# The first expert's rows by a product of the tokens on chip with a selection matrix, in place of a gather through DRAM and transposes

## The chip, the cores and the metric

The kernel runs on one core of a Trainium2 chip, as one program in one launch. The metric is the device time of one execution in microseconds. Engines are named as in the profile: PE (matmuls; PEld is its weight load), DVE, ACT, POOL and SP, which issues most of the DMAs. A profile covers one execution, and its times are counted from the start of that execution's span.

## The reference, cut to what matters

Two blocks run one after the other on 512 tokens of 1024 channels: a mixer block of two layers, and a second block with two kinds of attention and a mixture of experts. Only the mixture of experts and the step that leads into it matter here.

```python
x = x + jnp.concatenate([o_dil, o_fox], axis=-1) @ w_out[layer]
h2 = _rmsnorm(x, ffn_norm[layer]).reshape(B * T, D)
...
group_probs = jax.nn.softmax(group_logits, axis=-1)
g1, g_idx = lax.top_k(group_probs, 1)
sel = jnp.take_along_axis(expert_logits, g_idx[:, :, None], axis=1)[:, 0]
top_v, top_i = lax.top_k(sel, TOP_K_IN_GROUP)
g2 = jax.nn.softmax(top_v, axis=-1)
...
for e in range(N_EXPERTS):
    he = jax.nn.silu(xt @ w_gate[e]) * (xt @ w_up[e])
    y = y + combine[:, e:e + 1] * (he @ w_down[e])
```

There are 32 experts in 4 groups. Each token goes to two experts of one group. An expert has two matrices of 1024 x 256 (gate, up) and one of 256 x 1024 (down), in float32: 3 MB per expert, about 100 MB in all.

## The kernel before, in words

**Instructions and their order.** The program is traced in Python. A scheduler then orders the instructions of each engine by what they depend on and by the order in which they were traced. Inside a block `manual_schedule` the instructions of the engines named keep the order in which they are traced (others may be put between them). `issue_after(ins)` puts all that is traced in it behind `ins` on the engine of `ins`. Each engine, and each DMA queue, works in order.

**The step into the experts** is `second_out` (L1458). The 512 tokens are four tiles of 128 tokens on the partitions. For each tile a generator `tile(t)` (L1482) makes the two halves of the output projection (`pfo`), adds them into the tokens `xk` on chip, sums the squares, transposes the tokens (`turn8`, L1500) for the router, takes `rs`, the tile's inverse root mean square (`rsq`, L1501), and makes the router's logits (`plg`, L1505). Then ACT writes the scaled tokens in another channel order to `h` (L1509), which goes to the DRAM tensor `h2d` (L1510). `route_tile` (L1550) picks the two experts of each token (`both` has a 1 for each) on DVE. PE then counts how many earlier tokens chose the same expert (`prank`, L1583 and L1584), which gives the token's place among the expert's rows, and sums the table of tokens by place and expert in PSUM (`ppos`, L1592). The steps of the four tiles are interleaved by hand: `SO[0]` in free order, `SO[1] = (3,0,3,1,3,2,3,1,2,3,2,3)` under `manual_schedule` for PE, so PE's last steps are `prank` of tile 3, `ppos` of tile 2, `ppos` of tile 3.

**From the tables to the experts.** `route_end` (L1633) reads the table of the first three experts (`tables_of`, L1598 and L1599), which gives `tok`, the token numbers in the order of the rows. `sort_experts` (L1640) is traced under `issue_after(self.tabled.ins)` (L1991), so its DVE part comes behind those two instructions. It counts the tokens of each expert (`pcnt`), forms keys (L1652), compares all pairs (`sx`, L1654), sums to a `rank` (L1656), and makes `order` (L1667), the order in which experts 3 to 31 are taken. SP reads `order` from memory (L1965) before it can issue any load of a weight of these experts, since the expert's number is part of the address (`w_of`, L1959). Experts 0 to 2 have fixed places; their weights are asked for earlier (L1637, L1638 and, in the attention, L1770).

**An expert.** POOL gathers the expert's rows from `h2d` (`ex_gather`, L1814) into one of two buffers `xg`. PE transposes them in eight parts (L1798). ACT (first two experts, L1804) or DVE scales each part by the norm's weight `fwc` into `exT`. PE makes gate and up (`ex_gu`, L1831: 2 x 2 x 8 matmuls of 128x128; the trace counts two records for each float32 matmul), and later the down projection (L1871, L1892). In `moe` (L1944) the gathers of experts 0 and 1 are issued first, then `turn(0)`, the gather of expert 2 (into the buffer of expert 0), and after that gate and up of expert 0 (`gu(0)`). Weights run ahead by five experts for gate and up (`LA`) and three for down (`WH`): there are 16 buffers of 512 KB in the rings and four more in the pool for every fifth expert.

**Where the tiles of this stretch lie on chip.** Each tile is rounded up to 32 bytes per partition. Pool `oT` holds (L1226 to L1233, L1353) `yT2` twice 16384 bytes, four small tiles of 32, `wr` 1152, `br` 160 and `oT` twice 2048: 38304 bytes. Pool `out2` (L1465) follows it, with `h2` and `x2T` (L1497, L1498). Both are released at the end of `second_out` (L1520, L1521), and pool `moe` (L1947) begins where `oT` began: `xg1` 4096, `exT` twice 4096, `io512` 2048, `cnt` and `key` 128 each, `ys` six times 4096, then `rank` (128), `order`, `psort`, `by` and others. `rank` so starts 39168 bytes behind the common start. A tile that lies over an older one waits for the last reader of the older one.

Of the kernel before, what the change touches and what calls it, by code (L numbers as in the profile page):

```python
# [10 lines left out]
F32 = mybir.dt.float32  # L11
# [4 lines left out]
OP = mybir.AluOpType  # L16
# [96 lines left out]
class K:  # L113
# [1344 lines left out]
    def second_out(self):  # L1458

        nc, I, sp = self.nc, self.I, self.sp  # L1460
        xk, yT, xp = self.xk, self.yT, self.xp
        self.ring.append(self.pool("experts1", side="right"))
        self.ep = self.pool("experts", side="right")
        rp = self.rp = self.pool("route", side="right")
        c = self.pool("out2")  # L1465
        self.wsl = self.ep.tile([128, 32 + NX], F32, name="wsl")
        self.scat = self.ep.tile([128, 32 + NX], U32, name="scat")
        self.tok = self.ep.tile([128, 32 + NX], U32, name="tok")
        self.exinfo = self.ep.tile([1, 1 + NX], I32, name="exinfo")
        self.order = self.ep.tile([1, NE - AH], I32, name="order")  # L1470
        self.h2d = self.dr.tile([512, 1024], F32, name="h2d")
        wo = I["w_out_2"][0].rearrange("(k p) n -> p k n", p=128)
        us = [[self.wunit(wo[:, 4 + 2 * j:6 + 2 * j, c0:c0 + 512], [128, 2, 512]) for j in range(2)] for c0 in (0, 512)]
        wr, br = self.wr, self.br

        self.fwc = self.ep.tile([128, 8], F32, name="fwc")
        nc.gpsimd.dma_start(self.fwc, I["ffn_norm_2"][0].rearrange("(p k) -> p k", k=8))
        self.xgs = [rp.tile([128, 1024], F32, name="xg0")]
        nc.gpsimd.memset(self.xgs[0], 0.0)
        R = self.R = self.route_setup(rp)  # L1480

        def tile(t):  # L1482

            x = xk[:, t, :]
            ss = sp.tile([128, 2], F32, name="h2s", bufs=2)
            for i, c0 in enumerate((0, 512)):
                p = self.pt("pfo") if i else self.pc("pfo")
                for k in range(4):
                    self.mm3(p, [y[:, 4 + k, t * 128:(t + 1) * 128] for y in yT], [x[:, k % 2, :] for x in us[i][k // 2]],
                             k == 0, k == 3)  # L1490
                o = xk[:, t, c0:c0 + 512]
                nc.vector.scalar_tensor_tensor(o, p, self.rsh[1][:, t:t + 1], o, op0=OP.mult, op1=OP.add)
                junk = self.op.tile([128, 512], F32, name="oT", tag="oT", bufs=2)
                nc.scalar.activation(junk, o, AF.Square, accum_out=ss[:, i:i + 1])
                yield
            rs = sp.tile([128, 1], F32, name="h2r", bufs=2)
            h = c.tile([128, 1024], F32, name="h2", tag="h2", bufs=2)  # L1497
            y = c.tile([128, 8, 128], F32, name="x2T", tag="x2T", bufs=2)  # L1498
            nc.vector.tensor_tensor(ss[:, 0:1], ss[:, 0:1], ss[:, 1:2], op=OP.add)
            self.turn8(y, x)  # L1500
            self.rsq(rs, ss[:, 0:1], 1.0 / D, EPS)  # L1501
            yield
            pl = self.pt("plg")[:, :36]
            for k in range(8):
                nc.tensor.matmul(pl, y[:, k, :], wr[:, k, :], start=(k == 0), stop=(k == 7))  # L1505
            nc.vector.scalar_tensor_tensor(R["lg"][:, t], pl, rs, br, op0=OP.mult, op1=OP.add)

            h3 = h.rearrange("p (k c) -> p k c", k=8)
            nc.scalar.activation(h3, x.rearrange("p (c k) -> p k c", k=8), AF.Copy, scale=rs)  # L1509
            nc.scalar.dma_start(self.h2d[t * 128:(t + 1) * 128, :], h)  # L1510
            yield from self.route_tile(t, R, rp)

        tiles = [tile(t) for t in range(4)]
        for t in SO[0]:
            next(tiles[t], None)
        with self.tc.manual_schedule(engines={mybir.EngineType.PE}):
            for t in SO[1]:
                next(tiles[t], None)
        self.route_end()
        c.release()  # L1520
        self.op.release()  # L1521


    def route_setup(self, c):
        nc = self.nc
        V = nc.vector
        R = {}
        io = R["io"] = c.tile([128, 128], F32, name="io")
        nc.gpsimd.iota(io, pattern=[[1, 128]], base=0, channel_multiplier=0, allow_small_or_imprecise_dtypes=True)
        R["rev"] = c.tile([128, 32], F32, name="rev")  # L1530
        V.tensor_scalar(R["rev"], io[:, :32], -1.0, 32.0, op0=OP.mult, op1=OP.add)
        jp = c.tile([128, 128], F32, name="jp2")
        nc.gpsimd.iota(jp, pattern=[[1, 128]], base=0, channel_multiplier=-1, allow_small_or_imprecise_dtypes=True)
        R["before"] = c.tile([128, 128], F32R, name="before")
        V.tensor_scalar(R["before"], jp, 0.0, None, op0=OP.is_gt)
        R["one"] = c.tile([128, 128], F32R, name="one2")
        V.tensor_scalar(R["one"], jp, -1000.0, None, op0=OP.is_ge)
        R["val"] = c.tile([128, 4, 2], F32, name="val")
        nc.gpsimd.iota(R["val"], pattern=[[128, 4], [512, 2]], base=-2048, channel_multiplier=1,
                       allow_small_or_imprecise_dtypes=True)  # L1540
        R["oh"] = c.tile([128, 4, 2, 32], F32, name="roh")
        R["both"] = c.tile([128, 4, 32], F32R, name="both")
        R["lg"] = c.tile([128, 4, 36], F32, name="lg")
        R["max"] = c.tile([128, 3, 4], F32, name="rmax")
        R["ps"] = c.tile([128, 4, 2], F32, name="rps")
        R["w"] = c.tile([128, 4, 2], F32, name="rw")
        R["pos"] = self.po("ppos")[:, :32]
        return R

    def route_tile(self, t, R, c):  # L1550
        nc = self.nc
        V = nc.vector
        rev = R["rev"]
        new = lambda n, name: c.tile([128, n], F32, name=name, tag=name, bufs=2)
        lg, oh, both = R["lg"][:, t], R["oh"][:, t], R["both"]
        gm, m0, m1 = (R["max"][:, i, t:t + 1] for i in range(3))

        def first(x, m, n, name):

            k, km = new(n, name + "k"), new(1, name + "m")  # L1560
            V.scalar_tensor_tensor(k, x, m, rev[:, :n], op0=OP.is_equal, op1=OP.mult)
            V.tensor_reduce(km, k, axis=AX.X, op=OP.max)
            return k, km

        gl = lg[:, 0:4]
        V.tensor_reduce(gm, gl, axis=AX.X, op=OP.max)
        k, km = first(gl, gm, 4, "gf")
        V.tensor_scalar(k, k, km, -1e30, op0=OP.is_lt, op1=OP.mult)
        el, rest, drop = new(32, "el"), new(32, "rest"), new(32, "drop")
        V.tensor_tensor_reduce(el.rearrange("p (g e) -> p g e", g=4), lg[:, 4:36].rearrange("p (g e) -> p g e", g=4),  # L1570
                               k[:, :, None].to_broadcast([128, 4, 8]), 1.0, -3e38, OP.add, OP.max, m0)
        k, km = first(el, m0, 32, "f0")
        V.tensor_scalar(drop, k, km, -3e30, op0=OP.is_equal, op1=OP.mult)
        V.tensor_tensor_reduce(rest, el, drop, 1.0, -3e38, OP.add, OP.max, m1)
        V.tensor_scalar(oh[:, 0], k, km, None, op0=OP.is_equal)
        k, km = first(rest, m1, 32, "f1")
        V.tensor_scalar(oh[:, 1], k, km, None, op0=OP.is_equal)
        V.tensor_tensor(both[:, t], oh[:, 0], oh[:, 1], op=OP.add)
        yield

        pr = self.pt("prank")[:, :64]
        for u in range(t):
            nc.tensor.matmul(pr[:, 0:32], R["one"], both[:, u], start=(u == 0), stop=False)  # L1583
        nc.tensor.matmul(pr[:, 0:32], R["before"], both[:, t], start=(t == 0), stop=True)  # L1584
        for k in range(2):
            x = new(32, "rx")
            V.tensor_tensor_reduce(x, pr[:, 0:32], oh[:, k], 1.0, 0.0, OP.mult, OP.add, R["ps"][:, t, k:k + 1])
        yield
        for k in range(2):
            oo = c.tile([128, 128], F32, name="oo", tag="oo", bufs=3)  # L1590
            V.tensor_scalar(oo, R["io"], R["ps"][:, t, k:k + 1], R["val"][:, t, k:k + 1], op0=OP.is_equal, op1=OP.mult)
            nc.tensor.matmul(R["pos"], oo, oh[:, k], start=(t == 0 and k == 0), stop=(t == 3 and k == 1))  # L1592
# [351 lines left out]
    def moe(self):  # L1944
# [37 lines left out]
            if e < NE:  # L1982
                X[e] = self.ex_turn(xgs[e % 2], mp, cap[e], e < 2)

        gather(0)
        gather(1)
        turn(0)
        gather(2)
        self.io512 = mp.tile([128, 512], F32, name="io512")
        nc.gpsimd.iota(self.io512, pattern=[[1, 512]], base=0, channel_multiplier=0, allow_small_or_imprecise_dtypes=True)  # L1990
# [202 lines left out]
```

## Time and profile before

| | |
|---|---|
| runs | 1412.39, 1417.26, 1419.44 us; median 1417.26 us |
| profiled execution | 1414.1 us, span 1412.3 us |
| mean granted PE clock | 0.97 |
| busy share of the span | PE 91%, DVE 66%, ACT 43%, POOL 22% |
| moved by DMA | 246 MB, mean 174 GB/s |

The profiled execution's own time is 1.8 us more than its span. The experts take from about 1105 us to the end. [...] A row of a timeline gives start, length, engine (SPq is SP's queue of DMA issues), line, operation, tile written <- tiles read, and in square brackets the idle time before it with what ended it.

### The profile page before, as it was taken

What the parts mean: (1) busy time and instruction counts of PE and PEld (TensorE: products, weight loads), DVE (VectorE), ACT (ScalarE), POOL (GpSimd) and SP (SyncE); (2) the same over time, 40 slices, a digit from 0 to 9 for tenths busy, and PEclk for the clock granted to TensorE, in tenths of its full rate; (3) what the DMA queues carried; (4) which work ended last, traced back from release to release, by engine and by line L of the source; (5) the groups of instructions that cost most, each with busy time, mean ns of one, the idle gap of its engine ahead of it and who ended that gap; (6) DMA issues with size and microseconds to landing.
All of it is one profiled execution on the core that took longest, in us unless ns stands there. A gap on an engine that the chain in (4) does not pass through costs nothing. (4 is left out here: it accounts for less than half of the span.)

```text
span 1412.3 us, 22313 instructions
## 1 busy us (share of the span) xinstructions
PE 1289.8 (91%) x7958; PEld 1021.3 (72%) x7958; DVE 939.0 (66%) x2062; ACT 611.6 (43%) x1197; POOL 312.4 (22%) x412
## 2 busy tenths in 40 slices
PE   4999999999989999899999999999999799998792
PEld 2888778877868788677877778787788776674350
DVE  5789998566643689998776463676766733534565
ACT  4553155445641474256574153777655211111122
POOL 5333032322220234133222020211110111111100
PEclk9999999999999999999998999999999799999996
DMA  9643355435132254416143356333333799999992
GB/s 342 161 129 108 102 147 159 132 99 182 60 135 61 91 127 150 139 46 166 39 124 109 140 173 172 96 82 128 97 127 118 255 389 387 369 373 375 391 401 91
DMA packets 166772, 246.18 MB, mean 174 GB/s; under 512 B 46788, under 2 KB 102810, under 8 KB 166660
## 3 DMA queue, kind: packets, MB, share of 16 engines
q1 hardware_dynamic: 161116, 234.95, 50.1%
q0 software_dynamic: 4864, 7.66, 2.0%
q10 hardware_dynamic: 680, 2.13, 0.4%
q8 instruction: 64, 1.05, 0.3%
q14 instruction: 48, 0.39, 0.1%
HBM read 220.69 MB, written 32.28 MB: 179 GB/s over the span
## 5 line engine op out<-in xcount | busy, mean ns | idle before, releaser
L185 DVE TENSOR_TENSOR wlo<-wraw,whi 128x1024 fp32r<-128x1024 f32 (+3 forms) x98 | 118.2, 1212 | 60.2 <-ACT whi L184 59.7
L184 ACT ACTIVATE whi<-wraw 128x1024 fp32r<-128x1024 f32 (+3 forms) x98 | 100.6, 1036 | 103.1 <-PE pout L223 42.9
L221 PE MATMUL pcm<-hTh,whi 128*128 128x256 f32 (+1 forms) x288 | 102.3, 355 | 9.2 <-DVE oa L531 4.3
L571 DVE SCALAR_TENSOR_TENSOR za<-zp,vec,za 128x783 f32<-128x783 f32 (+1 forms) x120 | 108.8, 914 | 0.5
L923 POOL TENSOR_SCALAR P<-P,ll 128x768 f32<-128x768 f32 (+1 forms) x80 | 73.7, 927 | 160.2 <-DVE ll L922 143.5
L223 PE MATMUL pcm<-hTh,wlo 128*128 128x256 f32 (+1 forms) x288 | 98.4, 342 | 0.1
L222 PE MATMUL pcm<-hTl,whi 128*128 128x256 f32 (+1 forms) x288 | 97.9, 340 | 0.0
L185 DVE TENSOR_TENSOR PTl<-pPT,PTh 128x512 fp32r<-128x512 f32 x104 | 70.3, 684 | 25.2 <-ACT PTh L184 24.7
L921 ACT ACTIVATE P<-pS,nm 128x768 f32<-128x768 f32 (+1 forms) x80 | 65.0, 816 | 36.6 <-DVE nm L919 30.4
L184 ACT ACTIVATE PTh<-pPT 128x512 fp32r<-128x512 f32 x104 | 60.7, 597 | 45.8 <-PE pPT L936 41.5
L1814 POOL DMA_INDIRECT xg<-h2d,tok x32 | 31.5, 986 | 214.2 <-PE pturn L1798 159.8
L1418 POOL TENSOR_SCALAR P<-P,l 128x384 f32<-128x384 f32 (+1 forms) x64 | 33.3, 536 | 184.6 <-DVE l L1417 167.5
L919 DVE TENSOR_REDUCE nm<-pS 128x1 f32<-128x768 f32 (+1 forms) x80 | 66.0, 843 | 9.6 <-PE pS L223 8.8
L221 PEld LDWEIGHTS pcm<-hTh,whi 128*128 128x128 f32 x288 | 54.8, 190 | 17.3 <-DVE oa L531 4.9
L221 PE MATMUL pcm<-hT0h,whi 128*128 128x512 f32 x144 | 59.5, 413 | 7.7 <-DVE oa L531 5.8
L936 PE MATMUL pPT<-ident,P 128*128 128x128 f32 x416 | 63.1, 280 | 1.0 <-DVE PTl L185 0.4
L968 POOL TENSOR_TENSOR oa<-oa,ot 64x256 f32<-64x256 f32 x40 | 37.4, 935 | 99.7 <-DVE ot L967 96.3
L223 PEld LDWEIGHTS pcm<-hTh,wlo 128*128 128x128 f32 x288 | 54.7, 190 | 6.5 <-DVE wlo L185 0.6
L222 PEld LDWEIGHTS pcm<-hTl,whi 128*128 128x128 f32 x288 | 54.9, 191 | 5.1 <-issue 0.5
L222 PE MATMUL pcm<-hT0l,whi 128*128 128x512 f32 x144 | 58.4, 406 | 0.0
L223 PE MATMUL pcm<-hT0h,wlo 128*128 128x512 f32 x144 | 58.4, 406 | 0.0
L221 PE MATMUL pS<-khi,qhi 96*128 96x256 f32 (+1 forms) x144 | 51.1, 355 | 4.3 <-ACT P L921 2.4
(521 smaller groups left out, 3633.0 us busy)
## 6 DMA issues: line engine op xcount, KB each, us to landing
wraw<-in_w_in_dram SPq DMA_DIRECT2D x56, 512.0 KB, 4.8
eraw<-in_w_expert_gate_dram SPq DMA_DIRECT2D x52, 512.0 KB, 10.8
eraw<-in_w_expert_up_dram SPq DMA_DIRECT2D x52, 512.0 KB, 11.3
wraw<-in_w_mod_dram SPq DMA_DIRECT2D x48, 512.0 KB, 6.0
wl<-in_w_expert_down_dram SPq DMA_DIRECT2D x32, 512.0 KB, 6.4
wh<-in_w_expert_down_dram SPq DMA_DIRECT2D x32, 512.0 KB, 10.8
wraw<-in_w_out_dram SPq DMA_DIRECT2D x24, 512.0 KB, 3.8
wraw<-in_w_expert_gate_dram SPq DMA_DIRECT2D x12, 512.0 KB, 13.5
```

Source lines behind the costliest of these rows:

```text
L184: nc.scalar.activation(hi, src, AF.Copy)
L185: return (eng or nc.vector).tensor_tensor(lo, src, hi.bitcast(F32), op=OP.subtract)
L221: mm(out, lhs[0], rhs[0], start=start, stop=False)
L222: mm(out, lhs[0], rhs[1], start=False, stop=False)
L223: mm(out, lhs[1], rhs[0], start=False, stop=stop)
L571: nc.vector.scalar_tensor_tensor(a[:, :nz], z[:, k:k + nz], cfw[:, i, k:k + 1], a[:, :nz], op0=OP.mult, op1=OP.add)
L919: nc.vector.tensor_reduce(nm, S, axis=AX.X, op=OP.max, negate=True)
L921: nc.scalar.activation(P, S, AF.Exp, bias=nm, accum_out=l)
L923: nc.gpsimd.tensor_scalar(P, P, l, 0.5, op0=OP.mult, op1=OP.mult)
L936: nc.tensor.transpose(p[:, jj, i * 128:(i + 1) * 128], Ps[i][:, (j + jj) * 128:(j + jj + 1) * 128], self.ident)
L968: nc.gpsimd.tensor_tensor(o, o, t, op=OP.mult)
L1418: nc.gpsimd.tensor_scalar(Ps[i], Ps[i], l[:, i:i + 1], 1.0, op0=OP.mult, op1=OP.mult)
```

## The change

For expert 0 the gather through `h2d` and the eight transposes are left out. Instead each tile makes a selection matrix `sel0[:, t]` (128 tokens x 128 places) on DVE: where the token's place for expert 0 equals the column's number it holds `rs` times 1 or 0 (whether the token chose expert 0), else 0. `rows(i)` multiplies the tokens `xk` on PE, as stationary operand with every eighth channel as a column, with `sel0`, and sums over the four tiles into two PSUM banks `x0`: 32 float32 matmuls of 128x128 with 128 columns, 16 in each `rows`. PE's order by hand becomes: ..., `prank` of tile 3, `ppos` of tile 2, `rows(0)`, `ppos` of tile 3, `rows(1)`. In `moe` ACT scales the eight parts of `x0` by `fwc` straight into `exT`. Gathers of experts 1 and 2 follow one another. `h2d` and the `h` of every tile stay, for the other experts. The tile `jp2` is laid into `roh`, which makes 512 bytes free, and `sel0` (2048 bytes) is the first tile of pool `out2`.

```diff
+        sel0 = c.tile([128, 4, 128], F32, name="sel0")
+        def rows(i):
+            p = self.x0[i].rearrange("p (k n) -> p k n", k=4)
+            for k in range(4):
+                for t in range(4):
+                    nc.tensor.matmul(p[:, k], xk[:, t, :].rearrange("p (c k) -> p k c", k=8)[:, 4 * i + k, :], sel0[:, t],
+                                     start=(t == 0), stop=(t == 3))
...
-            yield from self.route_tile(t, R, rp)
+            yield from self.route_tile(t, R, rp, rs, sel0[:, t])
...
         with self.tc.manual_schedule(engines={mybir.EngineType.PE}):
-            for t in SO[1]:
+            for t in SO[1][:-1]:
                 next(tiles[t], None)
+            self.x0 = self.ph("px0")
+            rows(0)
+            next(tiles[3], None)
+            rows(1)
...
+        R["oh"] = c.tile([128, 4, 2, 32], F32, name="roh")
-        jp = c.tile([128, 128], F32, name="jp2")
+        jp = R["oh"].rearrange("p a b c -> p (a b c)")[:, :128]
...
-        R["oh"] = c.tile([128, 4, 2, 32], F32, name="roh")
+        R["first"] = c.tile([128, 2, 4], F32, name="rfirst")
...
         V.tensor_tensor(both[:, t], oh[:, 0], oh[:, 1], op=OP.add)
+        f = R["first"][:, :, t:t + 1]
+        V.tensor_tensor(f[:, 0], both[:, t, 0:1].bitcast(F32), rs, op=OP.mult)
         yield
...
         nc.tensor.matmul(pr[:, 0:32], R["before"], both[:, t], start=(t == 0), stop=True)
+        V.tensor_copy(f[:, 1], pr[:, 0:1])
+        V.tensor_scalar(sel, R["io"], f[:, 1], f[:, 0], op0=OP.is_equal, op1=OP.mult)
...
-        gather(0)
         gather(1)
-        turn(0)
+        X[0] = mp.tile([128, 8, 128], F32, name="exT", tag="exT", bufs=2)
+        for k in range(8):
+            nc.scalar.activation(X[0][:, k], self.x0[k // 4][:, k % 4 * 128:k % 4 * 128 + 128], AF.Copy,
+                                 scale=self.fwc[:, k:k + 1])
         gather(2)
```

## Rows read from the trace of the kernel before

**Rows 1.** Stretches of the experts: us, busy (x instructions) of each engine, PEclk, DMA share, GB/s.
```profile
1105.00:1110.00 5.00, 0.48 (x3) 0.34 (x2) 4.42 (x14) 0.31 (x2) 2.97 (x2) 0.50 0.14 31
...
1115.00:1376.00 261.00, 243.42 (x1967) 161.02 (x1966) 121.75 (x261) 44.94 (x93) 35.32 (x37) 0.98 1.02 382
...
1300.00:1320.00 20.00, 14.97 (x120) 7.24 (x120) 7.16 (x15) 3.08 (x6) 1.86 (x2) 0.90 1.00 381
1320.00:1340.00 20.00, 13.56 (x108) 7.28 (x104) 11.81 (x18) 3.08 (x6) 1.86 (x2) 0.93 1.03 397
```
**Rows 2.** PE in the timeline, its last long wait.
```profile
1340.54 1.07 PE L1892 MATMUL pyf<-wh,eh 128*32 128x512 f32 x3 [6.02 <-DMA wh<-in_w_expert_down_dram]
```
**Rows 3.** SP's queue in the timeline: last load before the gap, first after it.
```profile
1092.06 0.47 SPq L1785 DMA_DIRECT2D wl<-in_w_expert_down_dram  x1
1113.50 0.94 SPq L1770 DMA_DIRECT2D eraw<-in_w_expert_gate_dram  x2
```
**Rows 4.** SP's waits: engine line <- what it waited for: us in total, times, longest.
```profile
SPq L1965 <- DVE order L1667: 19.6, 1, 19.6
```
**Rows 5.** DVE in the timeline, from the table to the order of experts.
```profile
1105.52 0.16 DVE L1598 TENSOR_SCALAR scat<-ppos 128x3 uint32<-128x3 f32 x1 [1.07 <-PE ppos L1592]
...
1107.33 1.03 DVE L1656 TENSOR_REDUCE rank<-sx 128x29 f32<-128x841 f32 x1
...
1111.96 0.16 DVE L1667 CAST order<-order 1x29 int32<-1x29 f32 x1
```
**Rows 6.** PE in the timeline around the gap.
```profile
1103.13 0.39 PE L1584 MATMUL prank<-both,before 128*128 128x32 f32 x1 [1.37 <-DVE both L1578]
1103.37 1.04 PE L1592 MATMUL ppos<-roh,oo 128*128 128x32 f32 x4
1104.22 0.37 PE L1648 MATMUL pcnt<-both,one 128*128 128x32 f32 x1
1104.44 1.04 PE L1592 MATMUL ppos<-roh,oo 128*128 128x32 f32 x4
1111.73 1.94 PE L1798 MATMUL pturn<-ident,xg 128*128 128x128 f32 x8 [6.25 <-DMA xg<-h2d,tok]
1113.46 7.81 PE L1831 MATMUL pgu<-exT,eraw 128*128 128x128 f32 x64
```
**Rows 7.** POOL in the timeline: the gathers of experts 0, 1 and 2.
```profile
1106.72 1.56 POOL L1814 DMA_INDIRECT xg<-h2d,tok  x1 [12.38 <-DVE key L1652]
1108.59 1.73 POOL L1814 DMA_INDIRECT xg<-h2d,tok  x1 [0.30 <-issue]
1113.94 0.99 POOL L1814 DMA_INDIRECT xg<-h2d,tok  x1 [3.63 <-PE pturn L1798]
```
**Rows 8.** PE in the timeline at the full clock: a table's matmuls, gate and up of expert 1.
```profile
1089.66 0.53 PE L1592 MATMUL ppos<-roh,oo 128*128 128x32 f32 x4
...
1123.69 7.39 PE L1831 MATMUL pgu<-exT,eraw 128*128 128x128 f32 x64
```
**Rows 9.** Stretches, PE alone: us, busy (x), PEclk, DMA share, GB/s; fall and rise of the clock.
```profile
1097.00:1097.50 0.50, 0.50 (x6) 0.93 1.06 360
1097.50:1098.00 0.50, 0.50 (x5) 0.50 0.94 360
...
1114.00:1114.50 0.50, 0.50 (x4) 0.50 0.17 25
1114.50:1115.00 0.50, 0.50 (x7) 1.00 0.83 123
```
**Rows 10.** ACT by line: x count | busy us, mean ns | idle before; tokens read with and without stride.
```profile
L1509 ACT ACTIVATE h<-xk,h2r 128x1024 f32<-128x1024 f32 x4 | 9.0, 2256 | 7.0 <-DVE h2r L242 7.0
...
L1933 ACT ACTIVATE fo<-xk 128x1024 f32<-128x1024 f32 x4 | 4.2, 1058 | 7.6 <-DVE xk L1921 7.5
```
**Rows 11.** DVE by line, 1060 to 1140 us: x count | busy us, mean ns | idle before.
```profile
L1591 DVE TENSOR_SCALAR oo<-io,rps,val 128x128 f32<-128x128 f32 x8 | 2.6, 354 | 0.0
...
L1499 DVE TENSOR_TENSOR h2s<-h2s 128x1 f32<-128x1 f32 x4 | 0.6, 152 | 0.0
```

More of the change, by code (lines that the diff above doesn't have):

```diff
@@ L1546, in route_setup, with route_tile @@
         R["w"] = c.tile([128, 4, 2], F32, name="rw")
+        R["first"] = c.tile([128, 2, 4], F32, name="rfirst")
         R["pos"] = self.po("ppos")[:, :32]
         return R
-    def route_tile(self, t, R, c):
+    def route_tile(self, t, R, c, rs, sel):
         nc = self.nc
```

## The prediction

> **What bounds the kernel now.** I read the view by stretches first, since the change lies at one place, between router and experts. From 1115 to 1376 us the DMA engines are busy with a share of 1.02 and move 382 GB/s [rows 1]. PE is busy 243 of those 261 us, which looks like a second bound, but from 1300 to 1340 us it stands idle for 5.0 and 6.4 us [rows 1], and the timeline names the cause: its last long wait, 6.02 us, is for a down weight [rows 2]. So the stream of expert weights sets the pace, and PE catches up with it before the end. What is moved is fixed, so the end moves with the start of that stream. In SP's queue there is no load between 1092.06 and 1113.50 us [rows 3], and SP's waits say why: 19.6 us for `order` on DVE [rows 4]. The DVE timeline gives the way to it: table (1105.52), `rank` (1107.33), `order` (done at 1112.12) [rows 5]. The gap on PE, 6.25 us until the gathered rows of expert 0 land [rows 6], is what meets the eye and what the change takes away; but it runs beside this chain and is not what the weights wait for.
>
> **Removed.** The gather of expert 0 on POOL (1.56 us of issue) [rows 7], PE's wait of 6.25 us and eight transposes of 1.94 us [rows 6]. The gather moved when DMA was nearly idle, share 0.14 [rows 1], so it gives the stream nothing. Gathers 1 and 2 move up on POOL's queue. Gather 2 was issued at 1113.94, after a wait for the transposes [rows 7], and so moved its 128 rows of 4 KB, 0.52 MB, inside the full stream; now it goes before. At 382 GB/s [rows 1] that takes **1.4 us** out of the stream. ACT's eight scaled copies stay eight.
>
> **Added on DVE.** Per tile two one-column operations (0.15 us each) and a 128x128 comparison (0.35) [rows 11], 0.65 us. Those of tiles 0 and 1 lie beside the projection's matmuls. Those of tile 2 come in front of tile 3's choice of experts, for which PE already waits (1.37 us before `prank`) [rows 6], so I let all of **0.65 us** count; lower bound 0. Tile 3's own come while PE makes the table of tile 2.
>
> **Added on PE, and where it stands.** Gate and up of an expert are 32 float32 matmuls of 128x128 with 128 columns, 64 records in 7.39 us at the full clock [rows 8]: 0.115 us a record. `rows(0)` and `rows(1)` are 32 records each. [...] Which clock holds? It fell at 1097.5, amid narrow matmuls of the router, and rose at 1114.5, 2.8 us after PE began on the transposes and went on with gate and up without a break [rows 6, 9]. I take the same 2.8 us from the start of `rows(0)`. [...]
>
> The sum, in the time of the profiled execution:
> - `ppos` of tile 2 began at 1103.37 and took 1.04 [rows 6]; with 0.65 us of delay it ends at 1105.1, where `rows(0)` begins.
> - `rows(0)`: 12 records in 2.8 us, 20 at 0.115: 5.1 us, to 1110.2.
> - `ppos` of tile 3, queued behind it on PE: 0.53, to 1110.7. Before it ended at 1105.48 [rows 6]. The table, and with it all that `issue_after` holds behind it on DVE, is 5.2 us later.
> - `rows(1)`: 3.7 us, to 1114.4.
> - `rank` would now start at about 1112.5. But it lies on `sel0`: by the sizes in the code `sel0` takes bytes 38304 to 40352 behind the common start of the pools and `rank` starts at 39168. So the instruction that was free at 1107.33 [rows 5] waits for the last matmul of `rows(1)`, 1114.4: **7.1 us** later, and everything behind it on DVE with it.
> - `order` and the first load follow at the old distance: 1113.50 becomes 1120.6. Less 1.4 us for gather 2: the end comes **5.7 us later**.
>
> Gate and up of expert 0 start at about 1114.8 (one scaled copy of some 0.4 us behind `rows(1)`) against 1113.46 [rows 6], and run at the full clock, 7.39 us in place of 7.81 [rows 6, 8]: PE is 0.9 us later. DVE's later work, the table of the router's weights among it, also comes some 7 us later, and PE may wait for it behind gate and up of expert 0; both are covered by the 11.5 us in which PE waits between 1300 and 1340 us [rows 1]. Without that cover they would come on top, 0.9 us and at most 7.
>
> 1414.1 + 5.7 = 1419.8 us for the profiled execution. The median of the three runs is 3.2 us above it, so the forecast is **1423.0 us**, 0.40% more. A measurement of this kernel can tell some 0.5%, 7.1 us, from no change. Own range of this case: with the full clock throughout and `rank` not held back, the table ends at 1109.3, +3.9 - 1.4 = +2.5 us; with the low clock until the table and the full one after, `rows(1)` ends at 1117.2, +9.9 - 1.4 = +8.5.
>
> **Rivals.**
> - *The products run at half pace throughout* (slower). The stationary operand takes every eighth channel of `xk`. ACT reads the same tokens in the same pattern in 2256 ns, without stride in 1058 [rows 10]. If PE's weight load is slowed as much, a record takes some 0.23 us at the full clock; the same comes out if the clock doesn't rise. `rows(0)` 7.4, table 1.04, `rows(1)` 7.4 from 1105.1: 1120.9, so `rank` 13.6 us later and the end 12.2: 1426.3, 1429.5 against the median. It decides from about 0.14 us a record: 64 records then cost 1.5 us more than at 0.115, and the end passes the 7.1 us. Against it: ACT is another engine, and the rise of the clock is a row. [...]
> - *The stream of weights is not the bound* (no change). Then the end follows PE, +0.9 us: 1415.0, 1418.2 against the median. For it: PE is 93% busy from 1115 us on [rows 1]. Against: the wait of 6.02 us [rows 2].
> - *The scheduler draws the other engines' orders anew* (faster). Only PE's order in this block is by hand. If stores, gathers and selections fall so that PE's 11.5 us of idleness [rows 1] vanish, and the loads are not the bound, the end comes 11.5 - 0.9 = 10.6 us earlier: 1403.5, 1406.7 against the median. Against it: it needs both, and PE's own wait can't gain above what rows cost: from 1105.5 to 1113.46 PE can win 8 us [rows 6], and the products alone take 7.4 at the full clock.
> - *The change doesn't do what it says:* the gather of expert 0 is gone by the diff; I give it nothing.
>
> **How the numbers follow.** Forecast 0.58: most of its own range is within 7.1 us, so 0.38 no change and 0.20 slower. Half pace 0.27, slower. Not the bound 0.07, no change. Orders anew 0.08, faster. Together: faster 0.08, same 0.45, slower 0.47. The range: at the low end the case without the bound, 1418.2, less 4 us (the lowest of the three runs stands 4.9 below their median), 1414; at the high end half pace, 1429.5, and some 3.5 us for the runs' spread, 1433. Outside lie the faster rival and a tail of half pace.
>
> **What would show it.** `order` written at about 1119 us in place of 1112, the first load of expert 3 at 1120.6, and DVE idle before `rank` until the second product's last matmul: each step of the sum. 32 records of the second product within 3.7 us, and the four records of tile 3's table within 0.5: the pace. A share of 1.0 of DMA from some 1122 us to the end: the bound. It would be wrong if the first load comes no later, if `rank` is not held, or if the loads come late and the end doesn't.

## The result, and the profile after

The changed kernel takes 1427.32 us (median of 5 runs, 1426.07 to 1431.65) against 1417.05 us for the kernel before beside it (5 runs): a ratio of **1.0093** (95% interval 1.0076 to 1.0110), 13.2 us more. The ratio compares all runs of both kernels and is not the quotient of the two medians, which lie 10.3 us apart; where us are given for a ratio, here and below, they are that ratio times the median of the kernel before. The forecast was 1423.0 us, 0.40% more; the time lies in the range, near what the rival "half pace throughout" gave (1429.5 us).

The profiled execution took 1431.01 us, with a span of 1429.2 us. The first view is PE's timeline, to be held against [rows 6].

```profile
1104.31 0.39 PE L1601 MATMUL prank<-both,before 128*128 128x32 f32 x1 [0.88 <-DVE both L1593]
1104.55 1.04 PE L1612 MATMUL ppos<-roh,oo 128*128 128x32 f32 x4
1105.40 7.83 PE L1489 MATMUL px<-sel,xk 128*128 128x128 f32 x32
1113.07 0.53 PE L1612 MATMUL ppos<-roh,oo 128*128 128x32 f32 x4
1113.44 7.85 PE L1489 MATMUL px<-sel,xk 128*128 128x128 f32 x32
1121.04 0.26 PE L1668 MATMUL pcnt<-both,one 128*128 128x32 f32 x1
1121.15 7.39 PE L1851 MATMUL pgu<-exT,eraw 128*128 128x128 f32 x64
...
1356.40 1.07 PE L1912 MATMUL pyf<-wh,eh 128*32 128x512 f32 x3 [6.51 <-DMA wh<-in_w_expert_down_dram]
```

PE's gap of 6.25 us [rows 6] is gone, and two blocks of 32 records (`px`) stand in its place, 7.8 us each. The last matmul of the count of tokens (`pcnt`) has come to lie behind the second block; no order by hand fixes its place. The last long wait for a down weight is still there, 6.51 us, and comes 15.9 us later than in [rows 2].

Next, DVE on the way to the order of experts, as in [rows 5].

```profile
1113.64 0.16 DVE L1618 TENSOR_SCALAR scat<-ppos 128x3 uint32<-128x3 f32 x1 [7.73 <-PE ppos L1612]
...
1121.36 0.19 DVE L1670 COPY cnt<-pcnt 128x32 f32<-128x32 f32 x1 [7.26 <-PE pcnt L1668]
...
1122.88 1.03 DVE L1676 TENSOR_REDUCE rank<-sx 128x29 f32<-128x841 f32 x1
...
1127.43 0.16 DVE L1687 CAST order<-order 1x29 int32<-1x29 f32 x1
```

DVE stands idle twice, 7.73 us for the table behind the first block and 7.26 us for the count behind the second. From `rank` on nothing holds it: 6.09 us to the first load of expert 3 (SP's queue, next fence), 6.17 before [rows 3, 5].

```profile
1128.97 0.94 SPq L1790 DMA_DIRECT2D eraw<-in_w_expert_gate_dram  x2
```

By stretches (us, busy and instructions of PE, PEld, DVE, ACT and POOL, PEclk, which is the granted PE clock as a share of its full speed, DMA share, GB/s):

```profile
1105.00:1115.00 10.00, 10.00 (x46) 10.00 (x46) 1.33 (x9) 1.14 (x4) 0.15 (x1) 0.82 0.00 0
1115.00:1129.00 14.00, 14.00 (x98) 14.00 (x98) 7.61 (x21) 1.72 (x7) 3.48 (x4) 1.00 0.16 43
1131.00:1392.00 261.00, 238.62 (x1889) 153.55 (x1889) 120.34 (x257) 42.48 (x83) 35.22 (x37) 0.96 1.02 382
```

The same 261 us of full DMA as in [rows 1], at the same 382 GB/s, only later; ahead of them the DMA engines move nothing for 10 us and 43 GB/s over the next 14. Where the time went is told best from PE's `prank` of tile 3, a step ahead of both products (1103.13 before, 1104.31 after); over all profiles here it starts between 1100.60 and 1105.26, and counting from it leaves that scatter out. From there the first load of expert 3 is 14.3 us later, PE's gate and up of expert 0 6.5 us, and the last wait 14.7 us. Of the 16.9 us by which the two spans differ, 1.2 lie ahead of that point and 1.0 behind the last wait.

How fast the products run is seen from PE alone (stretches of 1 us: busy and records, PEclk, DMA share, GB/s), and from PE's weight loads by form (x count | busy us, mean ns | idle before).

```profile
1106.00:1107.00 1.00, 1.00 (x6) 0.50 0.00 0
...
1110.00:1111.00 1.00, 1.00 (x6) 1.00 0.00 0
...
1120.00:1121.00 1.00, 1.00 (x6) 1.00 0.75 299
```
```profile
L1489 PEld LDWEIGHTS px<-sel,xk 128*128 128x128 f32 x64 | 15.4, 335 | 0.0
L1851 PEld LDWEIGHTS pgu<-exT,eraw 128*128 128x128 f32 x70 | 8.0, 192 | 0.0
```

A stretch counts every record that reaches into it, so six a stretch stand for the 4.2 a microsecond of 32 records in 7.6 us, and they are six at 0.50 as at 1.00: the clock rose between 1108 and 1109 us (0.68 in that stretch), about where the forecast had it, and the products didn't get faster. A load of their stationary operand takes 335 ns, one of gate and up 192.

### The profile page after: what moved, and what is told of

It reads as the page before. It is cut to its first block, busy times and chain, and to the rows that moved or that the text cites. A ratio compares the mean times of both kernels' runs of the same rounds, so it can differ in the third digit from the quotient of the medians.

```text
span 1429.2 us, 22432 instructions
## 1 busy us (share of the span) xinstructions
PE 1307.2 (91%) x8014; PEld 1036.1 (72%) x8014; DVE 940.2 (66%) x2074; ACT 610.8 (43%) x1197; POOL 308.9 (22%) x411
## 6 DMA issues: line engine op xcount, KB each, us to landing
eraw<-in_w_expert_up_dram SPq DMA_DIRECT2D x52, 512.0 KB, 11.5
wh<-in_w_expert_down_dram SPq DMA_DIRECT2D x32, 512.0 KB, 11.2
```

## The experiments

All were timed in five rounds beside the kernel before (medians of before: 1415.88, 1414.72 and 1415.44 us in the three sets: the runs from e1 to e4, e6 to b1, and b2 to e9). This table collects, for each, the profile's start of the first load of expert 3 and of PE's gate and up of expert 0, and of PE's last wait for a down weight, each counted from `prank` of tile 3 and then less the same distance before (10.37, 10.33 and 237.41 us from [rows 2, 3, 6]). All are in us.

| kernel | first load | PE's start | last wait | ratio to before (95%) |
|---|---|---|---|---|
| the change | +14.3 | +6.5 | +14.7 | 1.0093 (1.0076 to 1.0110) |
| e1, no stride | +8.0 | +0.2 | +6.9 | 1.0047 (1.0031 to 1.0063) |
| e2, count first | +13.9 | +7.3 | +14.0 | 1.0087 (1.0073 to 1.0100) |
| e3, and `sel0` away | +13.9 | +7.3 | +15.2 | 1.0089 (1.0074 to 1.0105) |
| e4, and table first | +14.3 | +7.7 | +14.5 | 1.0085 (1.0071 to 1.0098) |
| e6, and exponentials first | +0.9 | +7.7 | +6.9 | 1.0055 (1.0037 to 1.0072) |
| e7, and no stride | +0.9 | +2.5 | +1.2 | 1.0007 (0.9993 to 1.0022) |
| b1, before, order late | +8.6 | +0.1 | +8.1 | 1.0059 (1.0039 to 1.0079) |
| b2, before, PE late | 0.0 | +7.4 | +7.2 | 1.0043 (1.0030 to 1.0057) |
| b3, before, both late | +8.6 | +7.3 | +10.7 | 1.0085 (1.0070 to 1.0100) |
| e9, e7 by tile | -0.1 | -3.1 | +1.5 | 1.0011 (0.9999 to 1.0022) |

For b2 and b3 PE's start is that of the second making of gate and up, taken as the first one's start and 7.39 us.

**e1: the stationary operand without stride.**

```diff
-  xk[:, t, :].rearrange("p (c k) -> p k c", k=8)[:, 4 * i + k, :], sel0[:, t],
+  xk[:, t, (4 * i + k) * 128:(4 * i + k + 1) * 128], sel0[:, t],
```

> The stationary operand of the products takes 128 neighbouring channels of the tokens in place of every eighth (so the channels of expert 0's rows stand in another order; this part of the computation is changed). Theory (the stride halves the pace): 0.115 us a record at the full clock in place of 0.24, the second product in 3.7 us in place of 7.85, the first in 5 to 6 because it starts at the low clock. The count's last matmul and rank come free some 6.4 us earlier, the first load of expert 3 at about 1122.6 in place of 1128.97, and the end 6 us earlier than with the change, about 1421. Rival (the pace has another cause, the moving operand or the accumulation over four tiles): the products stay at 7.8 us each and the end at 1427.

1421.77 us, ratio 1.0047: half of the loss is gone, as the theory had it. What e1 leaves out is the matching order of channels in gate and up, so expert 0 is not computed as in the reference; the instructions are those of the change, and e7 has the order that fits. PE's timeline of e1, and its weight loads of the products:

```profile
1106.35 5.53 PE L1489 MATMUL px<-sel,xk 128*128 128x128 f32 x32
1111.72 0.53 PE L1612 MATMUL ppos<-roh,oo 128*128 128x32 f32 x4
1112.08 3.82 PE L1489 MATMUL px<-sel,xk 128*128 128x128 f32 x32
1115.66 0.26 PE L1668 MATMUL pcnt<-both,one 128*128 128x32 f32 x1
```
```profile
L1489 PEld LDWEIGHTS px<-sel,xk 128*128 128x128 f32 x64 | 9.1, 230 | 0.0
```

Without the stride the blocks take 5.53 and 3.82 us, the second runs at 0.12 us a record, and the same loads take 230 ns in place of 335. So at 1.00 the pace is the stride's, not the clock's, and it cost 6.3 us on the first load and, as the difference of the two ratios, 0.46% of some 1416 us, 6.5 us, on the end.

**e2, e3, e4: the waits on the way to `order`, taken away one after the other.** e2 lays the count's matmuls ahead of the first block, e3 also makes `sel0` later, so that it lies elsewhere than `rank`, and e4 puts both blocks behind the table.

```diff
+            self.pcnt = self.pt("pcnt")[:, :32]
+            for u in range(4):
+                nc.tensor.matmul(self.pcnt, R["one"], R["both"][:, u], start=(u == 0), stop=(u == 3))
...
-        sel0 = c.tile([128, 4, 128], F32, name="sel0")
...
+            if "sel0" not in R:
+                R["sel0"] = c.tile([128, 4, 128], F32, name="sel0")
...
-            rows(0)
             next(tiles[3], None)
+            rows(0)
             rows(1)
```

> The four matmuls that count the tokens of each expert stand in PE's order by hand ahead of the first product, instead of one of them behind the second. Theory (two holds lie over each other, the count and the place of the selection matrix under rank): the count is copied right behind the table, at about 1114, but rank waits for the last matmul of the second product, about 1121.4; first load of expert 3 at about 1127.4, 1.5 us earlier, the end 1 to 2 us earlier, 1426. Rival (the count alone holds the order of the experts): first load 7.4 us earlier, 1121.6, and the end 7 us earlier, 1420.

> As the run with the count first, and the selection matrix lies behind the other tiles of its pool, where rank, order and the tiles made on the way to order don't lie on it. Theory: rank follows the comparison at once; what is left is the table behind the first product. First load at about 1121.6, 7.4 us earlier than with the change, gate and up of expert 0 still at 1121; the end 7 us earlier, 1420. Rival (the end follows PE, whose gate and up of expert 0 begin 7.7 us later than before): nothing is gained, 1427.

> As the run before, and both products stand behind the table of tile 3 on PE. Theory (the end moves with the first load of expert 3, not with PE): the table is done at about 1106, the first load at about 1114.8, 14 us earlier than with the change and 1 later than before; the products take as long as with the change, so gate and up of expert 0 begin at about 1121.5, 8 us later than before; the end is that of before within 3 us, 1414 to 1420. Rival (the end follows PE): no gain, 1427.

The ratios are 1.0087, 1.0089 and 1.0085: none of the three gains anything that can be told, though each removes its wait. In e2 the first load comes 0.4 us earlier, where the theory had 1.5. The theories of e3 and e4, an end at 1420 and at 1414 to 1420, missed; the rivals' 1427 came out, but not for the rivals' reason, since the first load didn't move either and so neither run tells whether the end follows PE. The DVE timelines of e2, e3 and e4, in this order, show what came next each time.

```profile
1111.09 0.18 DVE L1672 COPY cnt<-pcnt 128x32 f32<-128x32 f32 x1
...
1118.50 1.03 DVE L1678 TENSOR_REDUCE rank<-sx 128x29 f32<-128x841 f32 x1 [5.90 <-PE px L1489]
```
```profile
1116.29 1.03 DVE L1679 TENSOR_REDUCE rank<-sx 128x29 f32<-128x841 f32 x1
...
1123.43 0.17 DVE L1641 TENSOR_REDUCE g<-gx 128x4 f32<-128x16 f32 x1 [6.11 <-ACT gx L1639]
```
```profile
1105.70 0.16 DVE L1623 TENSOR_SCALAR scat<-ppos 128x3 uint32<-128x3 f32 x1 [1.42 <-PE ppos L1617]
...
1107.52 1.03 DVE L1679 TENSOR_REDUCE rank<-sx 128x29 f32<-128x841 f32 x1
...
1122.23 0.17 DVE L1641 TENSOR_REDUCE g<-gx 128x4 f32<-128x16 f32 x1 [13.68 <-ACT gx L1639]
...
1125.79 0.16 DVE L1690 CAST order<-order 1x29 int32<-1x29 f32 x1
```

In e2 the count is there early, and `rank` waits instead for the last matmul that reads `sel0`, the overlap in memory that the prediction named. In e3 `rank` is free before the second block ends, and DVE then stands at `g`, the sum of the router's exponentials, which is no part of the order of experts but comes ahead of `order` in DVE's queue. In e4 the table and `rank` come 0.6 us later than before the change, counted from `prank`, and the one wait that is left is 13.68 us long. ACT's timeline, of the kernel before and then of e4, says why the exponentials (`gx`) are late.

```profile
1106.09 0.21 ACT L1614 ACTIVATE gx<-gx 128x16 f32<-128x16 f32 x1 [4.88 <-DVE gx L1612]
...
1112.86 2.18 ACT L1804 ACTIVATE exT<-pturn,fwc 128x128 f32<-128x128 f32 x8 [6.46 <-PE pturn L1798]
```

```profile
1113.35 1.14 ACT L2011 ACTIVATE exT<-px,fwc 128x128 f32<-128x128 f32 x4 [12.89 <-PE px L1488]
1120.96 1.14 ACT L2011 ACTIVATE exT<-px,fwc 128x128 f32<-128x128 f32 x4 [6.47 <-PE px L1488]
1121.97 0.23 ACT L1639 ACTIVATE gx<-gx 128x16 f32<-128x16 f32 x1
```

Before, the exponentials ran ahead of the eight scaled copies; in the change these copies wait for the products, and the exponentials stand behind them in ACT's queue. Four holds lie over one another: the table, the count, `sel0` and the exponentials.

**e6: the exponentials ahead of the copies on ACT.**

```diff
+        with tc.issue_after(self.tabled.ins):
+            self.route_exp(mp)
...
-        for k in range(8):
-            nc.scalar.activation(X[0][:, k], self.x0[k // 4][...], AF.Copy, scale=self.fwc[:, k:k + 1])
+        with tc.issue_after(self.exped.ins):
+            for k in range(8):
+                nc.scalar.activation(X[0][:, k], self.x0[k // 4][...], AF.Copy, scale=self.fwc[:, k:k + 1])
```

> As the run with the table first, and the two exponentials of the router's weights stand ahead of the scaled copies of expert 0's rows in ACT's queue. In the run before them DVE stood 13.68 us at the sum of these exponentials, which lay behind the copies, and these behind the second product. Theory (the end moves with the first load of expert 3, not with PE): nothing on the way to order waits for a product any more; first load at about 1114.5, 13 us earlier than in the run before, gate and up of expert 0 as late as there, at about 1121; the end at 1414 to 1419, level with before. Rival (the end follows PE, which is 8 us late): 1424 or more.

1422.36 us, ratio 1.0055. The first load is now at its old place (+0.9 us), and yet 7.8 us of loss remain, with PE 7.7 us late on expert 0. So the theory (level with before) failed here, and the rival, that the end follows PE, was the nearer one. SP's waits of e6 between 1105 and 1170 us (total, times, longest), and a stretch of 30 us of it:

```profile
SPq L1798 <- PE pgu L1859: 19.1, 12, 3.7
```
```profile
1125.00:1155.00 30.00, 30.00 (x227) 23.80 (x229) 14.77 (x54) 5.39 (x14) 4.92 (x5) 1.00 0.93 320
```

The same views of the kernel before:

```profile
SPq L1770 <- PE pgu L1831: 6.3, 4, 3.5
```
```profile
1125.00:1155.00 30.00, 30.00 (x227) 21.42 (x229) 10.95 (x27) 3.69 (x7) 5.32 (x6) 1.00 1.03 396
```

SP waits three times as long for gate and up to free weight buffers, and in these 30 us the loads bring 76 GB/s less: 2.3 MB, which at 382 GB/s are 6.0 us of the stream. PE was 6.9 us further behind than the loads.

**e7: also without the stride,** with gate and up of expert 0 loaded in the channel order that fits it.

```diff
-            v = w.rearrange("(p k) n -> p k n", k=8)
+            v = w.rearrange("(p k) n -> p k n", k=8) if i else w.rearrange("(k p) n -> p k n", k=8)
```

> As the run before, and the products take 128 neighbouring channels; so that the result is the same, gate and up of expert 0 are loaded in that order of channels and the copies scale by the norm's weight in that order. Theory: both products in 9.5 us in place of 15.4, gate and up of expert 0 at about 1115; first load where it is in the run before, and the end level with it within 3 us. Rival (the end follows PE): 6 us earlier than the run before.

1415.26 us (12 runs), ratio 1.0007: level with the kernel before. Against e6 that is 0.48%, some 6.8 us, with the first load where it was: the rival's 6 us, and not the theory's end within 3 us of e6. Both blocks together take 10.22 us, the first load is 0.9 us late and PE 2.5 us.

**b1, b2, b3: the kernel before, with the order late, with PE late, and with both.** b1 has eight more comparisons on DVE ahead of `rank`; b2 makes gate and up of expert 0 twice; b3 does both.

```diff
+        for _ in range(8):
+            V.tensor_tensor(x, key[:, None, :]..., key[:, :, None]..., op=OP.is_gt)
...
-        for s in range(2):
+        for s in (0, 1, 0, 1) if self.twice else (0, 1):
```

> The kernel before, with the comparison of all pairs on the way to order made nine times in place of once: eight more DVE operations of 1.04 us, 8.3 us; PE's work is untouched. Theory: first load at about 1121.8 in place of 1113.50, the end 8.3 us later, 1424 beside 1416. Rival (the end follows PE): PE waits at most some us more for the table of the router's weights, and the end stays within 2 us of 1416.

> The kernel before, in which gate and up of expert 0 are computed twice in succession: PE does 64 more records, 7.4 us at the full clock, and everything behind them on PE is as much later, the release of the first weight buffers too. The order of experts and the first load of expert 3 are not touched. Theory 'the later of two' (the end goes with the later of the first load and of PE's start on the experts, since a late PE frees the ring's buffers late): the end comes 6 to 7.4 us later, a ratio of 1.004 to 1.005, SP waits for PE's gate and up more than 6.3 us in all between 1105 and 1170 us, and the loads move less than 380 GB/s between 1120 and 1160 us. Rival, as the prediction had it (PE's lateness is covered by its idleness between 1300 and 1340 us): no change, a ratio of 1.000 to 1.001.

> The kernel before with both delays at once: eight more comparisons on DVE on the way to the order of experts (8.4 us on the first load) and gate and up of expert 0 twice on PE (7.4 us). Theory 'the later of two': the end comes as much later as with the delay of the order alone, 8 to 9 us, a ratio of 1.006. Rival 'the two add up' (each delay costs by itself): some 15 us, a ratio of 1.011. Rival 'only the loads count': the same 8 us as the first theory; it is told from that by the run with PE alone late.

b1: 1424.36 us, ratio 1.0059, 8.4 us (5.5 to 11.2) for 8.6 us of delay: the end goes with the first load, one for one as far as this can be told. Its first load, and its last wait for a down weight:

```profile
1122.86 0.94 SPq L1772 DMA_DIRECT2D eraw<-in_w_expert_gate_dram  x2
```
```profile
1349.37 1.07 PE L1894 MATMUL pyf<-wh,eh 128*32 128x512 f32 x3 [6.04 <-DMA wh<-in_w_expert_down_dram]
```

b2: 1421.48 us, ratio 1.0043, 6.1 us (4.2 to 8.1): a late PE costs as well, with the loads begun on time, and the rival, which is the prediction's own cover, is out. In b2's profile the loads lose as much as in e6:

```profile
SPq L1770 <- PE pgu L1832: 18.7, 12, 3.9
```
```profile
1125.00:1155.00 30.00, 30.00 (x223) 24.01 (x225) 10.06 (x25) 5.39 (x14) 4.93 (x5) 1.00 0.93 320
```

b3: 1426.51 us, ratio 1.0085, 12.0 us (9.9 to 14.2). That is more than the later of the two (8.6) and less than their sum (15.9); by the last wait it is 10.7. In b3 the loads are 1.3 us later than PE and there is little for PE to stall: the same 30 us carry 392 GB/s.

```profile
1125.00:1155.00 30.00, 30.00 (x229) 23.58 (x227) 12.15 (x40) 5.38 (x14) 4.92 (x5) 1.00 1.02 392
```

So "the later of two" comes within 2.3 us of the runs in which one of them is later by 6 us or more, about as near as their intervals tell, and is 3.4 us short in b3 (2.1 by the last wait), where they are about level. Which of b3's later waits makes up the rest was not followed, and the cause stays open.

**e9: e7, with the product made tile by tile,** tile 0's part where PE waited before.

```diff
-            rows(0)
-            rows(1)
+            part(0, 0, 3)
+            next(tiles[2], None)
+            part(0, 3, 8)
...
+            for t in (1, 2, 3):
+                part(t, 0, 8)
```

> The mended version (contiguous stationary operand, table, count and exponentials ahead) with the product made tile by tile: three of tile 0's eight matmuls go where PE waits before the places of tile 2, five where it waits before those of tile 3, and only tiles 1 to 3 stand behind the table. Theory 'the later of two': in the mended version PE's start on expert 0 was 2.5 us late and the first load 0.9; now PE's start is 0 to 1 us late and the load 0.9 to 1.5, so the end is 0 to 1.5 us better than in the mended version: a ratio to the kernel before of 0.999 to 1.0005. Rival: PE's early matmuls delay the choice of places of tile 3 and with it everything, by up to 2 us: a ratio of 1.001 to 1.002.

1416.65 us (12 runs), ratio 1.0011: as e7, and no better than before. PE now begins expert 0 3.1 us earlier than before, counted from `prank`, and it brings nothing, since the loads don't begin earlier. From the transposes of tile 3 to its `prank` it takes 1.0 us more than in e7 (11.3 against 10.3 us), so the rival's delay is there too, and counted from these transposes the first load is 1.0 us later than before; in the ratio the two can't be told apart.

## Why the prediction was off in size

- **The bound** held for the change: the stream keeps its 382 GB/s, and where PE is on time the end moves with its start (b1: first load 8.6 us later, end 8.4). It is not all there is: with the loads on time and PE late (e6, b2) the stream itself falls to 320 GB/s for 30 us.
- **0.115 us a record once the clock is up** is the step that failed. The clock rose between 1108 and 1109 us, about where the prediction put it from [rows 6, 9] (1107.9); but `rows(0)` and `rows(1)` took 7.67 and 7.60 us from start to next start, not 5.1 and 3.7. e1 shows both halves: without the stride the blocks take 5.37 and 3.58 us by the same count, near the forecast's lengths; with it a record takes 0.24 us at either clock. This is the rival "half pace throughout", put at 0.27, and it was the case. The weight loads show it too: 335 ns a load with the stride, 230 in e1 without it, each over blocks that begin at 0.50 and end at 1.00; what makes a strided load longer was not shown. The prediction set the rival aside because ACT is another engine and the rise of the clock was a row; ACT's rows [rows 10], 2.1 times longer with the same stride, were the nearest ones and were right: 0.24 is 2.1 times 0.115. The 12 records in 2.8 us of the sum stand for 0.23 us a record at the low clock, an estimate that no run shows; at 0.50 a record took 0.24 us with the stride, and 0.22 without it in the transposes of expert 0 before the change (8 records from 1111.73 to 1113.46 us [rows 6]).
- **`rank` behind the second block** held as a time, but by another wait than the one named, and that is luck. Forecast were 7.1 us, of which 0.65 lay ahead of tile 3's `prank`; counted from `prank` it was 14.4 later in place of 6.45. The pace explains 6.3 of the difference (e1). The rest is the count: its last matmul lies behind the second block, which the prediction's steps didn't name, and DVE had to make key and comparison after it. From the start of the second block to `rank` it takes 9.44 us with the change, and 7.89 in e2, where the count is out of the way. So in the change DVE stood idle before `cnt` and not before `rank`, as the prediction's sign had it; e2 shows `sel0` itself holding `rank`, 5.90 us, once the count is gone. The exponentials behind ACT's copies were not seen either; they cost nothing in the change as it stands, and everything once the other three holds are out of the way (e4, 13.68 us on DVE).
- **0.65 us on DVE before tile 3:** from tile 3's transposes to its `prank` it took 10.11 us before and 10.26 after, so 0.15, nearer the lower bound of 0.
- **1.4 us for gather 2** can't be seen: from the first load to the last wait it is 227.0 us before, 227.4 after and 226.0 in e1, but also 226.5 in b1, whose gathers are those of before. No run shows this term.
- **"Covered by the 11.5 us in which PE waits"** is the second step that failed. PE was 6.5 us late, not 0.9, and b2 shows that 7.4 us of lateness cost 6.1 with the order on time. PE's idleness between 1300 and 1340 us is no store for it: the loss falls between 1125 and 1160 us, where SP waits for PE to free the buffers that the next loads go into. In the change itself this cost nothing that can be seen, because the loads were later still: between 1105 and 1170 us SP waits 0.6 us for PE's `pgu` (L1851), where it waited 6.3 before (L1831) and 18.7 in b2 (L1832).
- **The rival "not the bound"** fell with b1, since PE was on time there and the end came 8.4 us later; "orders anew" did not come, the end being later and not earlier.

With the half pace in place of the forecast's, the prediction's own steps give 12.2 us; measured are 13.2 (10.8 to 15.6). That they are so near is in part luck: the sum takes off the 1.4 us that no run shows, and leaves out the 1.5 us of the count; by the profile the last wait comes 14.7 us later.

## What to carry to other kernels

Size a matmul by its stationary operand's stride as well as by its columns and the clock: here a record took 0.24 us with the stride and 0.11 without it at 1.00 (e1). Where another engine's rows show a strided read at half pace, as ACT's did here (2256 ns against 1058), weigh that above a row without the stride. When work is put into a queue, list on every engine what stands behind it up to the instruction that starts the bounding stream: here four holds lay over one another, and taking away three of them gained nothing (1.0085 in e4, 1.0093 with the change). Don't count idleness of an engine late in a stage as cover for its lateness at the start where that engine frees the buffers of the stream that sets the pace: in b2 PE was 7.4 us late and the end came 6.1 us later. And closing PE's gap gained nothing here while that stream started no earlier: with the four holds and the stride out of the way (e7 1.0007, e9 1.0011) the change is level with the kernel before, not better.

## What the runs showed of the hardware

A float32 product of 128x128 with 128 columns whose stationary operand is read with a stride of 32 bytes took 0.24 us a record at a granted clock of 0.50 and of 1.00 alike (7.67 us for the first 32 records, during which the clock rose, and 7.60 for the second, at 1.00), and e1's second block without the stride 0.11 at 1.00 (3.58 us for 32), so at 1.00 the strided read, and not the clock, set its pace. Without the stride the clock decided. In e1 a stretch of 1 us holds or touches six records at 0.50, as with the stride, and eleven at 1.00, where with the stride it stays at six (PE's busy time and records, PEclk, DMA share, GB/s):

```profile
1108.00:1109.00 1.00, 1.00 (x6) 0.50 0.00 0
...
1110.00:1111.00 1.00, 1.00 (x11) 1.00 0.00 0
```

So here the stride cost little at 0.50 (0.24 us a record against 0.22 of the transposes in [rows 6]) and half the pace at 1.00 (0.24 against 0.11 in e1). e9 and e7 show the clock alone, in stretches of mostly unstrided matmuls of 128 columns. In e9 the clock fell at 1094, amid narrow matmuls of the router; the first products then fill PE's gaps, PE is busy without a break up to 1101, and there the clock rises to 1.00. In e7 PE stood idle 1.23 and 2.04 us before its last two `prank`s, the clock was 0.50 from 1099 to 1112, and half as many records came through. The first line is of e9, the second of e7:

```profile
1105.00:1110.00 5.00, 5.00 (x47) 1.00 0.09 22
```
```profile
1105.00:1110.00 5.00, 5.00 (x24) 0.50 0.00 0
```
